# Scores of two attention heads on separate halves of TensorE's rows, with the rounded and the low parts of q in tiles of their own

## The chip, the cores and the metric

The kernel runs on one core of one Trainium2 chip. The metric is the device time of one execution in microseconds (us); the time of a kernel is the median of its runs. One further execution was recorded by the hardware profiler, and all rows below come from it. The engines are named as in the profile: PE is TensorE's matmul, PEld its load of the stationary operand (it lies beside PE), DVE is VectorE, ACT ScalarE, POOL GpSimd, SP SyncE, from which the transfers are issued.

## The reference

A decoder layer on 512 positions of 2,048 channels. One projection of the modulated input gives q, k, v, two gates and the two halves of a gated convolution. Half of the layer is attention, 16 query heads of 64 channels over 4 key heads, each block of 128 queries looking at its own and the previous block of keys:

```python
scores = jnp.einsum('bnqhgd,bnkhd->bnhgqk', qb, kw) * (HEAD_DIM ** -0.5)
...
scores = jnp.where(valid[None, :, None, None], scores + bias, jnp.finfo(f32).min)
probs = jax.nn.softmax(jnp.concatenate([scores, sink], axis=-1), axis=-1)[..., :-1]
out = jnp.einsum('bnhgqk,bnkhd->bnqhgd', probs, vw)
```

The other half is a causal convolution of width 31 with a layer norm and a pointwise product. Both halves go through one output product, a residual and a last layer norm.

## The kernel before

**Halves.** Everything is float32. [...]

**Stages.** First the input is modulated and the convolution's inputs are projected, then k and v. Then for each of four groups `j` of four query heads the projections of q and of the attention gate follow (`project`, two PSUM tiles `prj`, 96 matmuls each), and after them the convolution's gate, the output product and the rest. On DVE the depthwise convolution (line 295, `cv`) is spread between the splits of the weights.

**q.** A group's q comes out of the projection as two PSUM tiles of 128 partitions, each with two heads of 64 channels one above the other. `q_out` makes one tile `qs` of 128 partitions for each head: its rounded half on one 64 partitions, its low half on the other 64. `kh` and `kl`, the halves of k, hold the same 64 channels twice, on the lower and the upper partitions.

**Scores.** With that, one matmul over all 128 rows of TensorE gives high plus low of q times the rounded k (line 411), a second one the same q times the low k (line 413), 256 keys wide each. A block (`attention`, one group and 128 queries) is 4 heads of 2 matmuls; there are 16 blocks, 128 score matmuls in all. DVE reads each head's scores out of PSUM with the bias and a running minimum (line 417), ACT takes the exponentials and scales them (422, 426), TensorE transposes (433), the transposed probabilities are split (174, 175), and `values` multiplies by v (443 over 128 columns of the stationary operand, 445 over 64).

**Order.** A block's three stages are put between the products of the next projections (`between`, STAGES = 0, 6, 9 steps of 12 matmuls), and the framework's scheduler orders each engine's queue from there. PSUM tiles of attention are named `att`; there are five of them, and a block uses two for scores, one or two for transposes and one for the values.

Of the kernel before, what the change touches and what calls it, by code (L numbers as in the profile page):

```python
# [18 lines left out]
P = 128  # L19
S = 512  # L20
# [24 lines left out]

# smalls: columns of one [128, n] array
SM_ADA = 0
# [6 lines left out]

# the first phase goes over the contraction chunks as they come; these pairs of
# output tiles (glu_a, glu_b) stay in PSUM, the others are summed part by part.
N_FIXED = 3
# [3 lines left out]

# microseconds of other work for the vector engine with each block of weights
N_WARM = 5
# [11 lines left out]
def plan():  # L75
    """The order of the first phase: the next chunk of h, unless the tensor engine would wait for weights."""
    done = {i: 0 for i in range(N_FIXED, NC8)}
    items, fixed, n_h = [("h", 0)], 0, 1
    dma, pe = 8.5, 11.0
    while n_h < NK:  # L80
        item = None
        i = min(done, key=lambda j: (done[j], j))
        n = min(n_h - done[i], PART[1])
        if pe - dma < LEAD:
            if fixed < n_h:
                item, dma, pe = ("fix", fixed), dma + 1.1, max(pe, dma + 2) + 3.9
                fixed += 1
            elif n >= min(PART[0], n_h):
                item, dma, pe = ("rot", i, done[i], n), dma + 0.37 * n, max(pe, dma + 2) + 1.3 * n
                done[i] += n  # L90
        if item is None:
            item, dma = ("h", n_h), dma + 6.6
            n_h += 1
        items.append(item)
    items += [("fix", k) for k in range(fixed, NK)]
    # what is left of each pair, most of it first
    rest = sorted(done, key=lambda j: (done[j], j))
    return items + [("rot", i, done[i], NK - done[i]) for i in rest if done[i] < NK]


def parts_of(k0, n):
    """At most four chunks to a block."""
    m = -(-n // 4)
    cuts = [k0 + n * a // m for a in range(m + 1)]
    return list(zip(cuts[:-1], cuts[1:]))


def w_in_blocks():
    """The blocks of w_in in the order of use: (first chunk, chunks, columns)."""
    blocks = []  # L110
# [12 lines left out]
def bucket_runs():  # L123
    """(bucket, first distance, one past the last distance) for distances 0..127."""
    max_exact = N_BUCKETS // 2
# [14 lines left out]
def build(tc, xT, x, c, wadaT, smalls, win, wpw, wout, relT, sinks, ln_g, ln_b, out):  # L140
# [11 lines left out]

    # ---- the activations of c, on all partitions
    ones = pp.tile([P, P], F32, name="ones")
# [17 lines left out]
    def split(raw, hi, lo, hi_engine=None):  # L172
        """hi + lo = raw, each with 12 significant bits."""
        nc.scalar.activation(hi, raw, AF.Copy)  # L174
        nc.vector.tensor_tensor(lo, raw, hi.bitcast(F32), op=ALU.subtract)  # L175
# [15 lines left out]
    def silu_c(pool, psp, tag):  # L191
        # the products of ones that come first set the tensor engine's clock
        warm = psp.tile([P, S], F32, name="warm", tag=tag)
# [5 lines left out]
        parts = [slice(i * S, (i + 1) * S) for i in range(4)]  # L199
        # the halves of c lie where the last chunks of h come later  # L200
        chl = [(hh[0:1, NK - 4 + i, :], hl[0:1, NK - 4 + i, :]) for i in range(4)]
# [12 lines left out]
    def ada(pool, cb, js, parts=1):  # L214
        """columns js of mod: for each, 128 outputs of the adaLN product, one per partition."""
        wa = [pool.tile([P, D], F32, name="wa", bufs=WA_BUFS) for j in js]
# [9 lines left out]

    # ---- phase 1: h and the GLU projections, chunk by chunk
    glu = {}
# [55 lines left out]
    def conv_steps():  # L284
        """the depthwise convolution, two chains at a time"""
        for i0 in range(0, NC8, 2):
# [14 lines left out]
    def take(gen, budget):  # L301
        """some of the work that fills the vector engine between the splits of the weights"""
        while budget > 0:
# [13 lines left out]

    # ---- phase 2: q, k, v, the gate, and attention
    def chain(*gens):
# [10 lines left out]

    # the negated bias of each head over the distance + 128; elsewhere the mask
    rel = p2.tile([16, N_BUCKETS], F32, name="rel", bufs=1)
# [58 lines left out]
    def attention(j, qs, sg, nb, n):  # L391
        """a block of queries of four heads, in three stages"""
        blk = slice(n * P, (n + 1) * P)
# [6 lines left out]
        def scores():  # L400
            # the negated scores, and after them the negated sink
            e = kept["e"] = p2.tile([P, GRP, 2 * P + 1], F32, name="e")
            least = p2.tile([P, GRP], F32, name="least")
            total = p2.tile([P, GRP], F32, name="total")
            nc.gpsimd.tensor_copy(e[:, :, nkeys], nsink[:, heads])
            for hp in range(2):
                sp = ps2.tile([P, S], F32, name="att", bufs=5)
                for r in range(2):
                    hd = 2 * hp + r
                    o = sp[:, r * 256:(r + 1) * 256]  # L410
                    nc.tensor.matmul(o, qs[hd][:, blk], kh[:, j, k0:k0 + 256], start=r == 0, stop=False,
                                     skip_group_check=True)
                    nc.tensor.matmul(o, qs[hd][:, blk], kl[:, j, k0:k0 + 256], start=False, stop=r == 1,
                                     skip_group_check=True)
                for r in range(2):
                    hd = 2 * hp + r
                    nc.vector.tensor_tensor_reduce(e[:, hd, :nkeys], sp[:, r * 256:r * 256 + nkeys],
                                                   nb[:, hd, nkeys - 1::-1] if nkeys < 256 else nb[:, hd, ::-1], 1.0,
# [20 lines left out]
        def values():  # L439
            pv = ps2.tile([P, S], F32, name="att", bufs=5)  # L440
            for half, (pth, ptl) in enumerate(kept["p"]):
# [3 lines left out]
                nc.tensor.matmul(pv[:HD, :], v[:, 0, :], ptl, start=False, stop=half == nh - 1, skip_group_check=True)  # L445
            # the products with the low halves of the values lie in the upper partitions
            low = p2.tile([HD, S], F32, name="low", bufs=1)
# [9 lines left out]

    # the stages of attention go between the products of the next projections
    stages = {}
# [7 lines left out]
    for j in range(NKV):  # L467
        qs = [p2.tile([P, S], F32R, name="qs", bufs=8) for _ in range(GRP)]
        def q_out(t, ps):
            for r in range(2):  # L470
                dst, rows = qs[2 * t + r], slice(r * HD, (r + 1) * HD)
                other = slice((1 - r) * HD, (2 - r) * HD)
                nc.scalar.activation(dst[rows, :], ps[rows, :], AF.Copy, scale=-(HD ** -0.5))
                nc.vector.scalar_tensor_tensor(dst[other, :], ps[rows, :], -(HD ** -0.5), dst[rows, :].bitcast(F32),
                                               op0=ALU.mult, op1=ALU.subtract)

# [5 lines left out]
        nb = p2.tile([P, GRP, 256], F32, name="nb")  # L482
        # [query, head, 255 - key]
        nc.sync.dma_start(nb, bass.AP(tensor=ext_d.tensor, offset=ext_d.offset + GRP * j * 384 + 1,
# [7 lines left out]

    # ---- phase 3: the gate of the convolution, and its layer norm
    def gc_out(j):
# [26 lines left out]
    def norm_steps():  # L521
# [27 lines left out]
        ps = colsum(tot)  # L549
        # 1 / sqrt(var + eps), and one Newton step: r (1.5 - 0.5 v r^2)  # L550
        nc.scalar.activation(tot, ps, AF.Sqrt, bias=eps, scale=1.0 / D_CONV)
# [12 lines left out]
        yield None  # L564
        # the normalised channels, through silu, take the place of the last chunks of h
        for i in range(NC8):
# [33 lines left out]
    def y_split(k0):  # L600
        # y of attention takes the place of the first chunks of h
        if k0 < 8:
# [7 lines left out]

    # ---- phase 4: the output product over the channels of attention
    def w_out_block(n, kp):
# [22 lines left out]

    # ---- phase 5: the pointwise product, its bias and gate; the attention half so far into the residual
    p5 = es.enter_context(tc.tile_pool(name="p5", bufs=1, reuse_waits="tile"))
# [56 lines left out]

    # ---- phase 6: the output product over the channels of the convolution, and the last layer norm
    def yh(k):
# [12 lines left out]

    # the weights of the last two column groups take the place of h  # L710
    def late_block(n, kp):
# [19 lines left out]
    for t in range(NB):  # L731
        ts_ = slice(t * P, (t + 1) * P)
        for n in (2, 3):
            # the last product in two parts, for what follows it to start early
            parts = [slice(0, HALF), slice(HALF, S)] if (t, n) == (NB - 1, 3) else [slice(0, S)]
# [21 lines left out]
def laid_out(x, c, w_ada, b_ada, w_in, rel_bias, sinks, conv_w, conv_b, conv_ln_g, conv_ln_b, w_pw, b_pw, w_out,  # L757
             ln_g, ln_b):
    x, w_in = np.asarray(x)[0], np.asarray(w_in)[0]
    cols = lambda v, n: np.asarray(v)[0].reshape(n, P).T  # noqa: E731  # L760
    cw = np.asarray(conv_w)[0].T.reshape(NC8, P, TAPS).transpose(1, 0, 2).reshape(P, NC8 * TAPS)
# [31 lines left out]
```

## Time and profile before

| | before |
|---|---|
| median of 3 runs (lowest to highest) | 789.35 us (788.3 to 790.66) |
| span of the profiled execution | 788.9 us |
| PE busy | 760.9 us, 96% |
| PEld busy | 628.9 us, 80% |
| DVE busy | 676.0 us, 86% |
| ACT busy | 341.8 us, 43% |
| stretch with the score matmuls | about 259 to 510 us |

The span is 0.45 us under the median and inside the runs' spread, so the rows can be set against the median with that difference. Matmuls are pipelined: the duration of one row (0.39 us for 512 columns) is longer than the distance to the next one's start (0.23 us). What a matmul costs is read from distances between starts.

### The profile page before, as it was taken

The page shows a single profiled execution, that of the slowest core. Times are in us where ns is not written, and L with a number is a line of the kernel's source. Part 1 is how long each engine was busy: PE and PEld are TensorE (multiplying, and loading weights), DVE is VectorE, ACT ScalarE, POOL GpSimd, SP SyncE. Part 2 cuts the span into 40 slices and gives each one's busy share as a digit, 9 for nine tenths or more (in the row PEclk, how much of TensorE's full clock was granted, in tenths as well). Part 3 has the DMA queues.
Part 4 walks back from the last instruction along what each step waited for, and adds up shares of the span by engine and source line. Part 5 has one row for each costly group of instructions (what it writes and reads, how often), then busy time and mean ns, then how long its engine had stood idle before and what let it go on. Part 6 is the DMA issues. An engine that isn't in the chain of part 4 may idle for free.

```text
span 788.9 us, 9718 instructions
## 1 busy us (share of the span) xinstructions
PE 760.9 (96%) x3522; PEld 628.9 (80%) x3522; DVE 676.0 (86%) x1101; ACT 341.8 (43%) x574; POOL 20.5 (3%) x30
## 2 busy tenths in 40 slices
PE   5999999999999999999999999999999799999994
PEld 4787888878898888888888888888878588888883
DVE  6888988959999999999999998579795539877797
ACT  4543333333242346656756756445473145433000
POOL 0000000000230000000000100000000000000000
PEclk9999999999999999999999999999999989999997
DMA  8999988513332232322321322367667633684033
GB/s 308 414 412 410 359 324 308 185 60 109 114 134 101 86 104 95 107 67 78 107 81 54 106 81 81 102 225 222 239 215 243 221 134 123 224 302 152 0 107 107
DMA packets 39089, 136.10 MB, mean 173 GB/s; under 512 B 4337, under 2 KB 6785, under 8 KB 34817
## 3 DMA queue, kind: packets, MB, share of 16 engines
q1 hardware_dynamic: 39042, 135.49, 49.2%
q8 instruction: 27, 0.44, 0.2%
q14 instruction: 20, 0.16, 0.1%
HBM read 131.26 MB, written 4.22 MB: 172 GB/s over the span
## 4 chain that ended last, share of the span: by engine, by line
PE 80%; DVE 9%; DMA 7%; issue 2%; ACT 0%; SPq 0%; DVEq 0%
PE prj L187 14%; PE prj L188 14%; PE prj L189 14%; DMA wa<-in_wadaT 6%; PE rot L187 5%; PE rot L189 5%; PE rot L188 5%; PE att L188 4%; PE att L189 4%; PE att L187 4%; PE fix L187 3%; DVE junk L588 3%; PE fix L188 3%; PE fix L189 3%; PE att L433 2%
## 5 line engine op out<-in xcount | busy, mean ns | idle before, releaser
L174 ACT ACTIVATE wh<-wr 128x1024 fp32r<-128x1024 f32 (+2 forms) x129 | 127.3, 997 | 203.5 <-PE prj L188 109.7
L187 PE MATMUL prj<-hh,wh 128*128 128x512 f32 x480 | 188.5, 393 | 0.0
L189 PE MATMUL prj<-hh,wl 128*128 128x512 f32 x480 | 187.6, 392 | 0.0
L188 PE MATMUL prj<-hl,wh 128*128 128x512 f32 x480 | 187.5, 391 | 0.0
L175 DVE TENSOR_TENSOR wl<-wr,wh 128x1024 fp32r<-128x1024 f32 (+2 forms) x129 | 147.3, 1145 | 27.5 <-ACT wh L174 27.1
L295 DVE SCALAR_TENSOR_TENSOR cv<-u,sm,cv 128x512 f32<-128x512 f32 x240 | 169.5, 743 | 0.8
L189 PEld LDWEIGHTS prj<-hh,wl 128*128 128x128 f32 x480 | 90.2, 188 | 19.4 <-issue 0.2
L187 PEld LDWEIGHTS prj<-hh,wh 128*128 128x128 f32 x480 | 90.2, 188 | 18.8 <-issue 0.2
L188 PEld LDWEIGHTS prj<-hl,wh 128*128 128x128 f32 x480 | 90.3, 188 | 18.1
L224 DVE CUSTOM_DVE_ANT_0 junk<-wa,cb,sm 128x2048 bf16<-128x2048 f32 (+1 forms) x32 | 72.9, 2279 | 2.6 <-DMA wa<-in_wadaT 2.6
L187 PE MATMUL rot<-hh,wh 128*128 128x512 f32 x160 | 62.2, 393 | 1.7 <-DVE acc L272 1.7
L188 PE MATMUL rot<-hl,wh 128*128 128x512 f32 x160 | 62.6, 391 | 0.0
L189 PE MATMUL rot<-hh,wl 128*128 128x512 f32 x160 | 62.5, 392 | 0.0
L188 PE MATMUL att<-wl,hh 128*128 128x512 f32 (+1 forms) x144 | 50.9, 354 | 6.7 <-DVE wl L175 6.7
L189 PE MATMUL att<-wh,hl 128*128 128x512 f32 (+1 forms) x144 | 50.2, 349 | 0.0
L187 PE MATMUL att<-wh,hh 128*128 128x512 f32 (+1 forms) x144 | 48.5, 349 | 0.0
L188 PE MATMUL fix<-hl,wh 128*128 128x512 f32 x96 | 38.2, 398 | 0.0
L187 PEld LDWEIGHTS rot<-hh,wh 128*128 128x128 f32 x160 | 30.3, 189 | 9.5 <-DVE acc L272 1.7
L189 PE MATMUL fix<-hh,wl 128*128 128x512 f32 x96 | 37.8, 394 | 0.0
L188 PEld LDWEIGHTS att<-wl,hh 128*128 128x128 f32 x144 | 28.0, 194 | 11.9 <-DVE wl L175 8.6
L189 PEld LDWEIGHTS rot<-hh,wl 128*128 128x128 f32 x160 | 30.1, 188 | 6.8 <-DVE wl L175 0.3
L188 PEld LDWEIGHTS rot<-hl,wh 128*128 128x128 f32 x160 | 30.1, 188 | 6.4
(163 smaller groups left out, 1179.3 us busy)
## 6 DMA issues: line engine op xcount, KB each, us to landing
wr<-in_win SPq DMA_DIRECT2D x68, 512.0 KB, 3.4
wa<-in_wadaT SPq DMA_DIRECT2D x30, 1024.0 KB, 8.6
wa<-in_wadaT SPq DMA_DIRECT2D x36, 512.0 KB, 5.0
wr<-in_wout SPq DMA_DIRECT2D x32, 512.0 KB, 4.6
wr<-in_win SPq DMA_DIRECT2D x24, 384.0 KB, 9.0
xt<-in_xT SPq DMA_DIRECT2D x16, 256.0 KB, 9.1
wr<-in_wpw SPq DMA_DIRECT2D x8, 512.0 KB, 3.3
xs<-in_x SPq DMA_DIRECT2D x16, 256.0 KB, 5.2
```

The costliest lines, as they stand in the source:

```text
L174: nc.scalar.activation(hi, raw, AF.Copy)
L175: nc.vector.tensor_tensor(lo, raw, hi.bitcast(F32), op=ALU.subtract)
L187: nc.tensor.matmul(ps, lh, rh, start=start, stop=False)
L188: nc.tensor.matmul(ps, lh, rl, start=False, stop=False)
L189: nc.tensor.matmul(ps, ll, rh, start=False, stop=stop)
L224: nc.vector.tensor_tensor_reduce(junk[:, part], w[:, part], cb[:, part], 1.0, first, ALU.mult, ALU.add, mod[:, j:j + 1])
L295: nc.vector.scalar_tensor_tensor(cv[i][:, :S], glu[i][:, j:j + S], w, cv[i][:, :S], op0=ALU.mult, op1=ALU.add)
L433: nc.tensor.transpose(pt[:, hd * P:(hd + 1) * P], kept["e"][:, hd, half * P:(half + 1) * P], ident)
L588: nc.vector.tensor_tensor_reduce(junk, wa, cb[:, hs], 1.0, dst if half else first, ALU.mult, ALU.add, dst)
```

## The change

`q_out` now writes one tile for each of the two PSUM tiles of q with both heads' rounded halves (`qs[2 * t]`, 128 partitions, one ACT instruction) and one with both heads' low halves (`qs[2 * t + 1]`, one DVE instruction). A score matmul takes 64 partitions of such a tile: head `r` of a pair lies on rows `64 r` to `64 r + 63`. A head's scores are now three matmuls over half of the rows: rounded q by rounded k, rounded q by low k, low q by rounded k; the fourth product, low q by low k, is no longer computed. The two heads of a pair alternate, and each writes a PSUM tile of its own (`sp[r]`), with the two pairs side by side in the columns.

```diff
-            for hp in range(2):
-                sp = ps2.tile([P, S], F32, name="att", bufs=5)
-                for r in range(2):
-                    hd = 2 * hp + r
-                    o = sp[:, r * 256:(r + 1) * 256]
-                    nc.tensor.matmul(o, qs[hd][:, blk], kh[:, j, k0:k0 + 256], start=r == 0, stop=False,
-                                     skip_group_check=True)
-                    nc.tensor.matmul(o, qs[hd][:, blk], kl[:, j, k0:k0 + 256], start=False, stop=r == 1,
-                                     skip_group_check=True)
+            sp = [ps2.tile([P, S], F32, name="att", bufs=5) for _ in range(2)]
+            for hp in range(2):
+                for a, b in ((qs[2 * hp], kh), (qs[2 * hp], kl), (qs[2 * hp + 1], kh)):
+                    for r in range(2):
+                        rows = slice(r * HD, (r + 1) * HD)
+                        nc.tensor.matmul(sp[r][:, hp * 256:(hp + 1) * 256], a[rows, blk], b[rows, j, k0:k0 + 256],
+                                         start=hp == 0 and b is kh and a is qs[0],
+                                         stop=hp == 1 and a is qs[3], skip_group_check=True)
+            for hp in range(2):
                 for r in range(2):
                     hd = 2 * hp + r
-                    nc.vector.tensor_tensor_reduce(e[:, hd, :nkeys], sp[:, r * 256:r * 256 + nkeys],
+                    nc.vector.tensor_tensor_reduce(e[:, hd, :nkeys], sp[r][:, hp * 256:hp * 256 + nkeys],
...
-            for r in range(2):
-                dst, rows = qs[2 * t + r], slice(r * HD, (r + 1) * HD)
-                other = slice((1 - r) * HD, (2 - r) * HD)
-                nc.scalar.activation(dst[rows, :], ps[rows, :], AF.Copy, scale=-(HD ** -0.5))
-                nc.vector.scalar_tensor_tensor(dst[other, :], ps[rows, :], -(HD ** -0.5), dst[rows, :].bitcast(F32),
-                                               op0=ALU.mult, op1=ALU.subtract)
+            nc.scalar.activation(qs[2 * t], ps, AF.Copy, scale=-(HD ** -0.5))
+            nc.vector.scalar_tensor_tensor(qs[2 * t + 1], ps, -(HD ** -0.5), qs[2 * t].bitcast(F32), op0=ALU.mult,
+                                           op1=ALU.subtract)
```

On PE, this is what stands at the second block of scores before the change; `att` with its number is a PSUM tile, `qs` with its number a tile of q.

```order
L189 MATMUL prj_2350<-hh_71,wl_2416 128x512
L411 MATMUL att_2458<-kh_1638,qs_2041 128x256
L413 MATMUL att_2458<-kl_1639,qs_2041 128x256
L411 MATMUL att_2458<-kh_1638,qs_2042 128x256
L413 MATMUL att_2458<-kl_1639,qs_2042 128x256
L411 MATMUL att_2465<-kh_1638,qs_2043 128x256
L413 MATMUL att_2465<-kl_1639,qs_2043 128x256
L411 MATMUL att_2465<-kh_1638,qs_2044 128x256
L413 MATMUL att_2465<-kl_1639,qs_2044 128x256
L187 MATMUL prj_2349<-hh_71,wh_2450 128x512
```

And this is the same block on PE with the change, without its neighbours among the projections; of two rows that follow each other the first takes the lower 64 partitions of `qs`, the second the upper 64.

```order
L412 MATMUL att_2458<-kh_1638,qs_2041 128x256
L412 MATMUL att_2459<-kh_1638,qs_2041 128x256
L412 MATMUL att_2458<-kl_1639,qs_2041 128x256
L412 MATMUL att_2459<-kl_1639,qs_2041 128x256
L412 MATMUL att_2458<-kh_1638,qs_2042 128x256
L412 MATMUL att_2459<-kh_1638,qs_2042 128x256
L412 MATMUL att_2458<-kh_1638,qs_2043 128x256
L412 MATMUL att_2459<-kh_1638,qs_2043 128x256
L412 MATMUL att_2458<-kl_1639,qs_2043 128x256
L412 MATMUL att_2459<-kl_1639,qs_2043 128x256
L412 MATMUL att_2458<-kh_1638,qs_2044 128x256
L412 MATMUL att_2459<-kh_1638,qs_2044 128x256
```

Eight rows have become twelve, and the two PSUM tiles take turns. In the changed program all 16 blocks stand like this, as one burst of 12 between projections; before, all but the first block stood as one burst of 8.

On DVE, this is where the first group's q is taken out of PSUM before the change (`qs`), between steps of the convolution (`cv`) and splits of weights (`wl`).

```order
L474 SCALAR_TENSOR_TENSOR qs<-prj,qs 64x512
L295 SCALAR_TENSOR_TENSOR cv<-u,sm,cv 128x512 x2
L474 SCALAR_TENSOR_TENSOR qs<-prj,qs 64x512
L295 SCALAR_TENSOR_TENSOR cv<-u,sm,cv 128x512 x2
L175 TENSOR_TENSOR wl<-wr,wh 128x1024
L474 SCALAR_TENSOR_TENSOR qs<-prj,qs 64x512
L295 SCALAR_TENSOR_TENSOR cv<-u,sm,cv 128x512 x2
L474 SCALAR_TENSOR_TENSOR qs<-prj,qs 64x512
```

With the change the same place on DVE reads:

```order
L473 SCALAR_TENSOR_TENSOR qs<-prj,qs 128x512
L295 SCALAR_TENSOR_TENSOR cv<-u,sm,cv 128x512 x3
L175 TENSOR_TENSOR wl<-wr,wh 128x1024
L295 SCALAR_TENSOR_TENSOR cv<-u,sm,cv 128x512
L473 SCALAR_TENSOR_TENSOR qs<-prj,qs 128x512
```

Four instructions on 64 partitions have become two on 128, and the convolution's steps have closed up around them.

## Rows read from the trace of the kernel before

**Rows 1.** The page: busy time of each engine with its share of the span and its instructions, and the first line of the chain that ended last (share of the span by engine).

```profile
PE 760.9 (96%) x3522; PEld 628.9 (80%) x3522; DVE 676.0 (86%) x1101; ACT 341.8 (43%) x574; POOL 20.5 (3%) x30
...
PE 80%; DVE 9%; DMA 7%; issue 2%; ACT 0%; SPq 0%; DVEq 0%
```

**Rows 2.** [...]

```profile
259.00:510.00 251.00, 251.00 (x1219) 208.98 (x1218) 234.49 (x446) 150.84 (x313) 7.69 (x14) 1.00 0.26 85
```

**Rows 3.** The view of waits for PE over the whole span: who waited for whom, us in total, times, longest.

```profile
PE att L188 <- DVE wl L175: 6.7, 4, 4.2
PE fix L187 <- ACT hh L245: 6.5, 1, 6.5
PE rot L187 <- DVE acc L272: 1.7, 2, 1.3
PE warm L195 <- DVE eps L161: 1.1, 1, 1.1
PE warm L211 <- ACT cb L208: 0.7, 1, 0.7
```

**Rows 4.** The timeline of PE around one block of scores: start, duration, engine, line, operation. The left-out lines go on in the same step.

```profile
309.08 0.39 PE L189 MATMUL prj<-hh,wl 128*128 128x512 f32 x1
309.31 0.28 PE L411 MATMUL att<-kh,qs 128*128 128x256 f32 x1
309.42 0.28 PE L413 MATMUL att<-kl,qs 128*128 128x256 f32 x1
...
310.14 0.28 PE L413 MATMUL att<-kl,qs 128*128 128x256 f32 x1
310.26 0.40 PE L187 MATMUL prj<-hh,wh 128*128 128x512 f32 x1
310.49 0.40 PE L188 MATMUL prj<-hl,wh 128*128 128x512 f32 x1
```

**Rows 5.** The view by lines with shapes kept apart: count, then busy us and mean ns of one, then idle time before. First the score matmuls, then loads of a stationary operand: of scores, of the values with 128 and with 64 columns, and two of the start of the program, with one row and with 128.

```profile
L413 PE MATMUL att<-kl,qs 128*128 128x256 f32 x64 | 16.1, 283 | 0.0
L411 PE MATMUL att<-kh,qs 128*128 128x256 f32 x64 | 16.0, 282 | 0.0
...
L411 PEld LDWEIGHTS att<-kh,qs 128*128 128x128 f32 x64 | 12.1, 190 | 0.7
...
L443 PEld LDWEIGHTS att<-pth,vhl 128*128 128x128 f32 x28 | 5.3, 188 | 1.7
L445 PEld LDWEIGHTS att<-ptl,vhl 128*64 128x64 f32 x28 | 3.8, 136 | 1.2
L195 PEld LDWEIGHTS warm<-ones 128*128 128x128 f32 x10 | 2.2, 329 | 1.0 <-DVE eps L161 1.0
L207 PEld LDWEIGHTS psc<-hl,ones_r 1*128 1x128 f32 x4 | 1.3, 316 | 0.2
```

**Rows 6.** The timeline of PE where the values and the transposes of two blocks meet; the line with x8 is a run of eight transposes, merged, 1.04 us from the first one's start to the last one's end. Beside it the mean of one transpose from the view by lines.

```profile
312.78 0.39 PE L189 MATMUL prj<-hh,wl 128*128 128x512 f32 x1
313.01 0.40 PE L443 MATMUL att<-pth,vhl 128*128 128x512 f32 x1
313.24 0.40 PE L445 MATMUL att<-ptl,vhl 128*64 128x512 f32 x1
313.48 1.04 PE L433 MATMUL att<-ident,e 128*128 128x128 f32 x8
...
L433 PE MATMUL att<-ident,e 128*128 128x128 f32 x112 | 15.1, 272 | 0.0
```

**Rows 7.** The timeline of PEld at an early place where PE had come to wait for a low half (0.20 us idle), so that two loads follow each other with nothing ahead of them.

```profile
24.28 0.19 PEld L188 LDWEIGHTS fix<-hl,wh 128*128 128x128 f32 x1 [0.20 <-DVE hl L247]
24.39 0.19 PEld L189 LDWEIGHTS fix<-hh,wl 128*128 128x128 f32 x1
```

**Rows 8.** The view by lines, shapes kept apart: the instructions of `q_out`, and two on 128 partitions of the same width.

```profile
L474 DVE SCALAR_TENSOR_TENSOR qs<-prj,qs 64x512 fp32r<-64x512 f32 x16 | 11.0, 688 | 0.5
L247 DVE TENSOR_TENSOR hl<-h,hh 128x512 fp32r<-128x512 f32 x16 | 11.0, 688 | 4.2 <-ACT h L246 4.2
...
L473 ACT ACTIVATE qs<-prj 64x512 fp32r<-64x512 f32 x16 | 9.5, 593 | 11.2 <-PE prj L189 5.6 <-DVE qs L474 5.3
...
L480 ACT ACTIVATE sg<-prj 128x512 f32<-128x512 f32 x8 | 4.7, 588 | 1.7 <-PE prj L189 1.7
```

**Rows 9.** Timelines of DVE and ACT between two blocks' scores: the split of transposed probabilities, the first read of scores, and the last scaling of probabilities before the transposes of 303.4 us.

```profile
306.94 0.68 DVE L175 TENSOR_TENSOR ptl<-att,pth 128x512 fp32r<-128x512 f32 x1
310.09 0.48 DVE L417 CUSTOM_DVE_ANT_0 e<-att,nb,nsink 128x256 f32<-128x256 f32 x1 [0.31 <-PE att L413]
...
290.22 1.28 ACT L426 ACTIVATE e<-e,total 128x128 f32<-128x128 f32 x4 [0.37 <-DVE total L424]
303.40 0.60 PE L433 MATMUL att<-ident,e 128*128 128x128 f32 x4
```

## The prediction

> **What bounds the kernel now.** I read the page first: PE is busy for 96% of the span and carries 80% of the chain that ended last [rows 1]. Then the view by stretches, for the 251 us in which all scores lie: PE is busy for every one of them, at the full clock [rows 2]. Then PE's waits: five in all, 16.7 us, and every one belongs to the start, the first phase or the output product; none is for scores, transposes or values [rows 3], and the score matmuls have no idle time before them [rows 5]. So between 259 and 510 us time is the sum of the distances between PE's starts and of nothing else. DVE, 234.49 of 251 us busy there, is close behind but is not waited for. What the change is worth is therefore what it does to those distances in 16 places.
>
> **What a block of scores takes now.** From the first score's start to the next projection's start the timeline has 310.26 - 309.31 = 0.95 us for 8 matmuls, 0.119 us each [rows 4]. Sixteen blocks: 15.2 us.
>
> **What a block takes after.** Twelve matmuls of the same 256 columns, each with its own load of 128 columns, alternating between the lower and the upper rows. No row of before has a matmul on half of the rows, so the price is bounded from both sides.
>
> The low bound is that the two of a pair run together and the pair goes at the pace of one matmul now: 6 x 0.119 = 0.71 us, 0.24 us less for each block, 16 x 0.24 = 3.8 us less in all. The high bound is that they don't overlap at all: 12 x 0.119 = 1.43 us, 0.48 more, 7.6 us more in all.
>
> Between them stands the load of the stationary operand. Its pace shows in two places. Where nothing was ahead of it, one load followed another after 0.11 us [rows 7]. And eight transposes, whose moving operand has only 128 columns, take 1.04 us with 0.272 for the last, so (1.04 - 0.272) / 7 = 0.110 us from one to the next [rows 6]. Both say that a load of 128 columns holds the load path for 0.11 us. That it is columns which count shows in 188 ns for 128 against 136 for 64; that rows don't shows at the start of the program, 316 ns for a load of one row against 329 for 128 [rows 5]. So a load of half of the rows should be no shorter. Today that hides: one load of 0.11 us lies beside one matmul of 0.119. After the change twelve loads stand where eight stood. If they go one after the other, as every pair of loads in this trace does, a block takes 12 x 0.110 = 1.32 us whatever the matmuls do: 0.37 more, 16 x 0.37 = 5.9 us more. I take this value: it is the one the nearest rows speak for, and it lies 1.7 us under the high bound.
>
> **Changing from full to half rows and back.** That happens twice a block, 32 times. The nearest row is the change between a stationary operand of 128 columns and one of 64 in the values: 0.23 us to it and 0.24 us from it, where two equal matmuls of 512 columns are 0.23 apart [rows 4, 6]. That is 0.01 us at most, 32 x 0.01 = 0.3 us. The other end is that the new shape waits until the matmul before has left the array: the rows give 283 ns for a score with the next one 119 later [rows 4, 5], so 0.164 us more, and 0.39 against 0.23 for a projection, 0.16. That is 32 x 0.164 = 5.3 us. I take the low end, 0.3 us, from the row that it is nearest to. [...]
>
> **Taking q out of PSUM.** Sixteen DVE instructions of 0.688 us on 64 partitions become 8 on 128. A 128-partition instruction of this width takes 0.688 as well, so DVE has 5.5 us less to do; ACT has 8 x 0.59 = 4.7 us less [rows 8]. PE waits for neither in this stretch [rows 2, 3], so I put both at nothing. What hides the work is PE itself. If DVE were the bound, these 5.5 us would be a gain.
>
> **New waits.** A block's two PSUM tiles are now both needed with its first pair, 0.48 us earlier than the second one was. The tiles of a block go round: five in use, five there. A block's scores come 12 us apart; the split that frees a transposed tile ended at 306.94 + 0.68 = 307.62, and the next scores began at 309.31 [rows 4, 9], while the same data's first use by the values was at 313.24, 5.6 us later [rows 6]. Probabilities lay ready at 291.5 for transposes at 303.4 [rows 6, 9]. The first DVE read of scores would come up to 0.4 us later in a block, which vanishes in 12 us. So no wait arises. The work behind attention on PE stands in the same order as before, and moves as a whole.
>
> **Sum.** 5.9 + 0.3 = 6.2 us on a span of 788.9: 795.1. The runs' median lies 0.45 us above the span, so 795.5.
>
> **Rivals.**
> Side by side, changes cheap: -3.8 + 0.3 = -3.5 us, 785.9. For it: the two of a pair use different rows and different PSUM tiles, and nothing in the program makes one wait for the other. Against it: it needs two loads within 0.119 us where the trace never shows two closer than 0.11. It decides as soon as loads to different rows overlap so far that a pair takes under 0.155 us (6 x 0.155 + 0.02 is today's 0.95). [...]
> Side by side, but drained at each change: -3.8 + 5.3 = +1.5 us, 790.9. [...]
> Loads in a row, or no overlap at all, and drained: 5.9 + 5.3 = 11.2 to 7.6 + 5.3 = 12.9 us more, 800.5 to 802.2. [...] Against it: the cheap change of rows 6.
>
> **Chances.** Loads in a row with cheap changes, up to no overlap at all (794 to 798): 0.35. Side by side and cheap: 0.25. Side by side and drained: 0.20. Both costs: 0.20. The forecast is the likeliest, 795.5 us, its own range 793.5 to 798. The range for all reaches from just under the first rival to the cheaper end of the last, 785.2 to 801. A measurement of this kernel tells about 0.3% (2.4 us) from no change: faster 0.25, within 0.3% 0.20, slower 0.55.
>
> **What would show it.** Right: starts of score matmuls 0.11 us apart all through a burst of 12, loads 0.11 apart, a burst of about 1.3 us, and the projections at both its ends at their usual 0.23. Side by side would show as two starts close together, then a pause, and a burst of 0.7 us. A drain would show as 0.16 us extra between the last projection and the first score, and again after the last. DVE's busy time in the stretch should fall by 5.5 us with no effect. I am wrong if PE waits for a score's PSUM tile or for q, or if the later stalls of the output product (6.7 us for weights, rows 3) come out differently because everything ahead of them has moved.

## The result, and the profile after

The changed kernel takes 795.73 us (median of 4 runs, 794.8 to 795.97) against 790.0 (4 runs, 788.3 to 790.82) before: ratio 1.007, 95% interval 1.0048 to 1.0093. The forecast of 795.5 us is met. Its reason is not: the loads do not go one after the other. What happened comes nearest to the rival "side by side, but drained at each change": a pair of scores every 0.117 us, and 0.195 us for each change of shape where that rival had 0.164; that the engine drains there is not shown. And 795.73 is at the upper end of what this kernel does; two further sets of runs (below) have medians of 793.97 and 794.34.

Busy time of each engine and the chain by engine, from the page of the changed kernel, answering [rows 1]:

```profile
PE 764.5 (96%) x3586; PEld 624.5 (79%) x3586; DVE 669.3 (84%) x1093; ACT 336.4 (42%) x566; POOL 16.0 (2%) x30
...
PE 80%; DMA 9%; DVE 8%; issue 2%; SPq 1%; ACT 0%; DVEq 0%
```

PE has 64 instructions more (16 blocks, 12 matmuls for 8) and is busy 3.6 us longer; DVE, ACT and PEld have less to do. The bound has not moved. Next, PE's timeline around one block of scores, answering [rows 4]: start, duration, engine, line, operation; x2 and x4 are runs of two and four with like operands, merged.

```profile
311.03 0.39 PE L188 MATMUL prj<-hl,wh 128*128 128x512 f32 x1
311.26 0.39 PE L189 MATMUL prj<-hh,wl 128*128 128x512 f32 x1
311.57 0.38 PE L412 MATMUL att<-kh,qs 64*128 64x256 f32 x2
311.80 0.28 PE L412 MATMUL att<-kl,qs 64*128 64x256 f32 x2
311.92 0.40 PE L412 MATMUL att<-kh,qs 64*128 64x256 f32 x4
312.15 0.28 PE L412 MATMUL att<-kl,qs 64*128 64x256 f32 x2
312.27 0.28 PE L412 MATMUL att<-kh,qs 64*128 64x256 f32 x2
312.48 0.50 PE L187 MATMUL prj<-hh,wh 128*128 128x512 f32 x1
312.82 0.40 PE L188 MATMUL prj<-hl,wh 128*128 128x512 f32 x1
```

Two matmuls begin together (x2), and behind the second pair the pairs follow each other at 0.12 us (311.80, 311.92). Twelve take 311.57 to 312.48, 0.91 us, where eight took 0.95. But at both ends there are gaps that the kernel before lacks: 0.31 from the last projection to the first score (0.23 before), 0.23 from the first pair to the second (0.12 between the others), 0.21 from the last pair to the projection (0.12 before), and 0.34 from that projection to the next (0.23 before).

The loads of the same burst, from PEld's timeline:

```profile
311.03 0.19 PEld L189 LDWEIGHTS prj<-hh,wl 128*128 128x128 f32 x1
311.57 0.19 PEld L412 LDWEIGHTS att<-kh,qs 64*128 64x128 f32 x2 [0.35 <-PE prj L188]
311.68 0.19 PEld L412 LDWEIGHTS att<-kl,qs 64*128 64x128 f32 x2
...
312.47 0.19 PEld L187 LDWEIGHTS prj<-hh,wh 128*128 128x128 f32 x1
312.58 0.19 PEld L188 LDWEIGHTS prj<-hl,wh 128*128 128x128 f32 x1
```

Two loads take together the 0.19 us that one takes: they run side by side, which no row of before had shown. And the first load after a change starts with its matmul (311.57 and 311.57, 312.47 and 312.48), where otherwise it runs ahead (311.68 for the matmul of 311.80). PEld sits idle for 0.35 us before it.

PE's waits, answering [rows 3]; the two at the start of the program (1.8 us) are as before:

```profile
PE fix L187 <- ACT hh L245: 7.0, 1, 7.0
PE att L188 <- DVE wl L175: 6.5, 3, 3.4
PE rot L187 <- DVE acc L272: 1.7, 2, 1.3
PE prj L188 <- DVE wl L175: 1.3, 1, 1.3
```

None is for scores or q. The fourth does not stand in [rows 3]; it lies in the output product, as the second does.

In these names `hh` and `wh` are rounded halves, which ACT writes (for the weights line 174), `hl` and `wl` low halves, the rest of the same numbers, which DVE writes (line 175); lines 187 to 189 are the three matmuls of one product, rounded by rounded and the two mixed ones.

**Where the time went.** The distance that holds all 16 blocks goes from the start of the first phase's last matmul (`rot`) to the start of the output product's first (`prj<-wh,hh`); I call it the stretch. Its two ends, from PE's timeline of before:

```profile
196.51 0.39 PE L189 MATMUL rot<-hh,wl 128*128 128x512 f32 x1
...
545.78 0.39 PE L187 MATMUL prj<-wh,hh 128*128 128x512 f32 x1
```

and of the changed kernel:

```profile
198.34 0.39 PE L189 MATMUL rot<-hh,wl 128*128 128x512 f32 x1
...
550.66 0.39 PE L187 MATMUL prj<-wh,hh 128*128 128x512 f32 x1
```

349.27 us have become 352.32: 3.05 us more. In it, taken to the whole microsecond, PE is busy throughout, before and after (first before, then after; columns, as in [rows 2]: length of the stretch, busy time and instructions of PE, PEld, DVE, ACT and POOL, TensorE's granted clock as a share of full speed, DMA share, GB/s):

```profile
196.00:545.00 349.00, 349.00 (x1739) 293.74 (x1739) 327.64 (x611) 188.50 (x364) 19.36 (x16) 1.00 0.32 105
```

```profile
198.00:550.00 352.00, 352.00 (x1804) 289.21 (x1803) 321.30 (x602) 183.18 (x356) 14.83 (x16) 1.00 0.31 104
```

So the 3.05 us are distances between PE's starts at the full clock (1.00 in both lines), and no wait. The pause before a burst is no wait in disguise either: it is 0.318 or 0.319 us in all 16 blocks, whatever semaphore the first score waits for, and also in the first block, where no wait stands directly before it. The profiled spans differ by 794.0 - 788.9 = 5.1: 3.05 here, 1.83 in that `rot` ended later, 0.2 behind. Whether the 1.83 belongs to the change the further runs tell.

The 3.05 by medians over the blocks, in us:

| distance between starts | before | after | difference |
|---|---|---|---|
| last projection to first score | 0.226 | 0.318 | +0.092 |
| first score to last | 0.832 | 0.697 | -0.135 |
| last score to next projection | 0.120 | 0.204 | +0.084 |
| that projection to the one behind it | 0.234 | 0.341 | +0.107 |
| sum | 1.412 | 1.560 | +0.148 |

Within the burst the first pair stands 0.222 ahead of the second, the others 0.117 apart: 0.105 of the 0.697 is the change of shape too, and without it the burst is 0.24 shorter. So a block gains 0.24 by the pairs and loses 0.092 + 0.105 + 0.084 + 0.107 = 0.39 by two changes, 0.195 each. Over 16 blocks: -3.8 + 6.2 = +2.4 us. The ten distances behind these add 0.039 a block (2.288 before, 2.327 after), 0.63 us; the remaining 0.05 is in no single place.

What the 0.107 and the 0.039 behind a burst are, a place of the kernel before shows where no rows change. At 51 us, at the full clock (1.00 from 50 to 54 us), PE's next load has had to wait for a low half, and so it starts with its matmul instead of ahead of it. PE's timeline there, and that load from PEld's:

```profile
51.16 0.39 PE L188 MATMUL rot<-hl,wh 128*128 128x512 f32 x1
51.43 0.50 PE L189 MATMUL rot<-hh,wl 128*128 128x512 f32 x1
51.77 0.40 PE L187 MATMUL rot<-hh,wh 128*128 128x512 f32 x1
52.01 0.40 PE L188 MATMUL rot<-hl,wh 128*128 128x512 f32 x1
...
51.42 0.19 PEld L189 LDWEIGHTS rot<-hh,wl 128*128 128x128 f32 x1 [0.30 <-DVE wl L175]
```

This matmul, too, lasts 0.50 us, the next one starts 0.34 after it, and the ten distances behind that add up to 2.326. It is the picture behind a burst, without a change of rows. At 28.73 us, in a second such place, the next matmul comes after 0.334 and the ten distances are 2.288: the 0.107 came with both loads, the 0.039 with one. So I read the 0.107 as the price of a load that could not run ahead; what the traces show of the change of rows itself is that the load is held back (PEld idle for 0.35 us before 311.57), and the pauses of 0.092 and 0.084 before it. The 0.105 behind the first pair looks like the same thing, but no row separates the two there.

### The profile page after: what moved, and what is told of

Same layout as the page of the kernel before. It is cut to its first block, busy times and chain, and to the rows that moved or that the text cites. A ratio compares the mean times of both kernels' runs of the same rounds, so it can differ in the third digit from the quotient of the medians.

```text
span 794.0 us, 9829 instructions
## 1 busy us (share of the span) xinstructions
PE 764.5 (96%) x3586; PEld 624.5 (79%) x3586; DVE 669.3 (84%) x1093; ACT 336.4 (42%) x566; POOL 16.0 (2%) x30
## 4 chain that ended last, share of the span: by engine, by line
PE 80%; DMA 9%; DVE 8%; issue 2%; SPq 1%; ACT 0%; DVEq 0%
PE prj L187 14%; PE prj L188 14%; PE prj L189 14%; DMA wa<-in_wadaT 8%; PE rot L187 5%; PE rot L189 5%; PE rot L188 5%; PE att L188 4%; PE att L189 4%; PE att L187 3%; PE fix L187 3%; PE fix L188 3%; PE fix L189 3%; DVE junk L587 3%; PE att L412 2%
## 5 line engine op out<-in xcount | busy, mean ns | idle before, releaser
L187 PE MATMUL prj<-hh,wh 128*128 128x512 f32 x480 | 190.5, 397 | 0.0
L423 ACT ACTIVATE e<-e,least 128x257 f32<-128x257 f32 (+1 forms) x64 | 30.2, 474 | 23.7 <-DVE least L418 23.6
```

The costliest lines, as they stand in the source:

```text
L187: nc.tensor.matmul(ps, lh, rh, start=start, stop=False)
L423: nc.scalar.activation(e[:, hd, :nkeys + 1], e[:, hd, :nkeys + 1], AF.Exp, bias=least[:, hd:hd + 1], scale=-1.0, accum_out=total[:, hd:hd ...
```

## Experiments

Theory, formed from these rows: pairs run side by side, and each change between full and half rows costs 0.19 us. Rivals: what is lost belongs to the single matmul or load (then it does not matter how many bursts there are), or to work outside PE (q's evacuation, or what lies behind attention). The number that decides is the length of the stretch, since it repeats far better than the time of a run. The expectations count a part of it, from the end of the v projection to the end of attention: 250.70 before, 253.75 after. It differs from the stretch by a constant.

| kernel | stretch, us | against before | time, ratio to before (95%) |
|---|---|---|---|
| before, and two repeats | 349.27, 349.27, 349.27 | | 1.0007 (0.9994 to 1.002), 0.9998 (0.9987 to 1.0009) |
| after, and two repeats | 352.32, 352.32, 352.32 | +3.05 | 1.007 (1.0048 to 1.0093), 1.0053 (1.0033 to 1.0074), 1.0049 (1.0031 to 1.0068) |
| after, bursts split | 358.72 | +9.45 | 1.0148 (1.0124 to 1.0172) |
| after, two blocks in a burst | 348.14 | -1.13 | 0.9993 (0.998 to 1.0006) |
| before, stages moved as in the row above | 349.11 | -0.16 | 0.9987 (0.9973 to 1.0001) |
| after, heads not alternating | 352.43 | +3.16 | 1.0056 (1.0034 to 1.0079) |
| after, one half of the rows only | 363.41 | +14.14 | 1.0183 (1.0163 to 1.0202) |
| before, with the new `q_out` | 349.36 | +0.09 | 1.0 (0.9982 to 1.0018) |

### Both kernels again

No edit but a comment in the kernel before; the changed one as it is.

> The kernel before, unchanged but for a comment, timed against itself. The first 1,192 matmuls of both kernels stand in the same order, yet in the profile of the changed one the end of the first phase came 1.82 us later (last matmul of the first phase's fixed tiles 171.4 us instead of 169.5). If that is chance of one execution, the start of this copy may lie anywhere between, and the ratio is 1.000 within 0.002. If it belongs to the program, this copy shows 169.5 again and the changed kernel 171.4.

> The changed kernel, unchanged, in five rounds. Shape theory: pairs run side by side (16 x 0.25 = 4.0 us less) and each burst pays about 0.39 us for going to half rows and back (16 x 0.39 = 6.3 us more); with what else the stretch shows 3.1 us in all, ratio near 1.004, if the 1.82 us at the start are chance. If they belong to the program, ratio 1.006 to 1.007 as in the first timing and the end of the first phase at 171.4 us again.

> The changed kernel once more, on the same chip as the three others. In the traces so far the stretch with attention is 3.05 us longer than before in both executions, the medians differ by 4.8 and 5.7. If the stretch is all, 1.004; if something outside it belongs to the change, 1.006 or more, with the place in the trace.

> The kernel before once more, for its trace. The means of spans differ by 4.3 us between before (787.8, 50 runs) and the changed kernel (792.1, 20 runs), of which the attention stretch has 3.05. If the rest lies in the output product, the stretch from the end of attention to the pointwise product is 143 to 143.5 us in an execution near the mean of before, against 144.6 to 145.1 in the three traces of the changed kernel; if it is spread, 144 or more.

The stretch repeats to 0.01 us, while times of one kernel spread over 4 to 6 us (790.92 to 797.1 in one set of ten). The first phase's last matmul starts at 198.34, 196.16 and 197.68 us in the three traces of the changed kernel, and at 196.51, 196.75 and 196.91 in those of before; one execution of the changed kernel is earlier than all of before, so the 1.83 us of the first profile are no fixed part of the change. Over the executions whose span was recorded the mean span is 787.9 us before (90) and 792.1 after (20): 4.2 more, of which the stretch explains 3.05. In the output product PE waits for low halves of weights (`att` and `prj`, line 188) for 6.7, 6.5 and 5.5 us in the three profiles of before, and for 7.8, 7.7 and 7.4 in those of after. That would be a further 1.4 us on average. But the time from the output product's first matmul to the pointwise product's first, of which the last expectation speaks, is 144.25, 144.92 and 142.21 us in the three profiles of before and 144.49, 144.88 and 144.46 in those of after. The third of before is even shorter there than expected, the other two are as long as the changed kernel's: where the rest lies is not settled. DVE, which writes those halves, itself waits between 540 and 620 us for transfers of the modulation's weights (17.7 us in the first profile of before, 16.5 in the first of after), so it is not simply that this wait grew; and the kernel with its scores on one half, which comes to this place 11 us later still, waits for 5.2 only.

### Twice as many bursts

```diff
-STAGES = (0, 6, 9)
+STAGES = (0, 0.5, 6, 9)
...
-        def scores():
+        def half_scores(hp):
...
+        def scores_a():
...
+            half_scores(0)
...
+        def scores_b():
+            half_scores(1)
...
```

The first pair of heads is multiplied where the block's burst stood, the second six projection matmuls later, with the reductions behind it.

> The changed kernel with each block's scores in two bursts of 6, one pair of heads each, with 6 projection matmuls between: 32 bursts instead of 16, same matmuls. Shape theory: 16 more goings and comings at 0.39 us, 6.3 us slower than the changed kernel, about 1.008. My forecast's load theory (0.11 us for each load, changes 0.01 us): 0.3 us slower, ratio to the changed kernel 1.000.

The same 192 score matmuls in 32 bursts of 6: the stretch grows by 6.40 us over the changed kernel's, 0.40 for each of the 16 bursts more. PE's timeline at half a block:

```profile
297.65 0.39 PE L189 MATMUL prj<-hh,wl 128*128 128x512 f32 x1
297.97 0.39 PE L407 MATMUL att<-kh,qs 64*128 64x256 f32 x2
298.20 0.28 PE L407 MATMUL att<-kl,qs 64*128 64x256 f32 x2
298.31 0.28 PE L407 MATMUL att<-kh,qs 64*128 64x256 f32 x2
298.52 0.50 PE L187 MATMUL prj<-hh,wh 128*128 128x512 f32 x1
298.86 0.40 PE L188 MATMUL prj<-hl,wh 128*128 128x512 f32 x1
```

The four long distances (0.32, 0.23, 0.21, 0.34) are those of the longer burst. Here the price hangs on the burst, not on the matmul.

### Half as many bursts

Two blocks' scores together, on the changed kernel; the same staging on the kernel before as a control. In the control the scores of two blocks are not one burst: only in the first pair of blocks do 14 of the 16 matmuls stand together, in the others one to seven projection matmuls stand between the parts. So it shows what moving the stages is worth, and not a burst of 16.

```diff
-        for n in range(NB):
-            for f, at in zip(attention(j, qs, sg, nb, n), STAGES):
-                stages.setdefault(hook[0] + 4 * n + at, []).append(f)
+        for m in range(0, NB, 2):
+            first, second = attention(j, qs, sg, nb, m), attention(j, qs, sg, nb, m + 1)
+            for f, at in sorted(((first[0], 0), (second[0], 0), (first[1], 4), (first[2], 6),
+                                 (second[1], 6), (second[2], 9)), key=lambda p: p[1]):
+                stages.setdefault(hook[0] + 4 * m + at, []).append(f)
```

> The changed kernel with the scores of two blocks in one burst of 24, transposes and values moved to steps 4, 6 and 6, 9 of the pair: 8 bursts instead of 16, same matmuls. Shape theory: 8 x 0.39 = 3.1 us faster than the changed kernel, so level with the kernel before or up to 0.8 us faster, if the moved stages wait for nothing new. Load theory: no difference to the changed kernel.

> The kernel before with the stages moved as in the run of two blocks to a burst, score matmuls over all rows. Shape theory: a matmul over all rows pays nothing at a burst's ends, so the stretch stays at 250.7 us and the ratio at 1.000; the run of two blocks to a burst was 1.1 us shorter in this stretch than before by its half rows. If moving the stages is itself worth something, this kernel gains what that one gained.

Eight changes in and out fewer took 4.18 us off the changed kernel's stretch, where 3.1 were expected. From PE's timeline:

```profile
285.83 0.39 PE L189 MATMUL prj<-hh,wl 128*128 128x512 f32 x1
286.15 0.38 PE L412 MATMUL att<-kh,qs 64*128 64x256 f32 x2
286.37 0.28 PE L412 MATMUL att<-kl,qs 64*128 64x256 f32 x2
...
287.56 0.28 PE L412 MATMUL att<-kh,qs 64*128 64x256 f32 x2
287.77 0.50 PE L187 MATMUL prj<-hh,wh 128*128 128x512 f32 x1
```

A burst of 24 pays the two changes once (medians 0.318, 0.206, 0.337) and lasts 1.411 from first score to last; 16 full-row matmuls would take 0.832 + 8 x 0.119 = 1.784. So a burst gains 0.37 and pays 0.092 + 0.086 + 0.103 = 0.28: 0.09 for each of 8, 0.74 us. With the control's 0.16 for the staging that is 0.90 of the 1.13 us by which it beats the kernel before. Of the 1.1 us that were not expected, 0.63 are the ten distances behind a block, which here take 2.288 us as in the kernel before; the rest is open. The gain over the kernel before is real in the stretch and below what the timing tells: its interval holds 1.

### Are the pairs needed, and do halves run apart?

In the first kernel the loops are swapped, so that a head's three matmuls follow each other on its half of the rows before the other head's; in the second every score matmul takes the lower half (its attention is therefore not the reference's).

```diff
-                for a, b in ((qs[2 * hp], kh), (qs[2 * hp], kl), (qs[2 * hp + 1], kh)):
-                    for r in range(2):
+                for r in range(2):
+                    for a, b in ((qs[2 * hp], kh), (qs[2 * hp], kl), (qs[2 * hp + 1], kh)):
```

```diff
-                        rows = slice(r * HD, (r + 1) * HD)
+                        rows = slice(0, HD)
```

> The changed kernel with the three matmuls of the lower head first and then the three of the upper one, in each half of a burst: the same 192 matmuls in the same 16 bursts, but neighbours now mostly use the same rows. Shape theory (halves on different rows run together, issue is in order): of 12 matmuls only the three pairs at the seams still overlap, 9 steps of 0.117 us instead of 6, 16 x 0.35 = 5.6 us slower than the changed kernel; 11.2 us if nothing overlaps at the seams. Load theory (each load 0.11 us whatever its rows): no difference to the changed kernel.

> The changed kernel with both heads of a pair taken from the lower 64 partitions, so that all 12 matmuls of a burst use the same half of the rows; the upper head's scores are then those of the lower one and the attention is not the reference's; the number and size of all operations is the changed kernel's. Shape theory, as the run without pairs has left it (each half of the rows takes its matmuls one after the other at 0.117 us, the two halves side by side whatever the order): 12 steps of 0.117 us in place of 6, 16 x 0.70 = 11.2 us longer than the changed kernel in the attention stretch (253.75 us), ends of the bursts unchanged. Load theory (0.11 us for each load, whatever the rows): no difference to the changed kernel.

The second came out as expected: 11.09 us over the changed kernel's stretch. PE's timeline of one block:

```profile
297.68 0.39 PE L189 MATMUL prj<-hh,wl 128*128 128x512 f32 x1
298.00 0.50 PE L412 MATMUL att<-kh,qs 64*128 64x256 f32 x2
298.34 0.39 PE L412 MATMUL att<-kl,qs 64*128 64x256 f32 x2
298.57 0.64 PE L412 MATMUL att<-kh,qs 64*128 64x256 f32 x4
...
299.28 0.40 PE L412 MATMUL att<-kh,qs 64*128 64x256 f32 x2
299.61 0.50 PE L187 MATMUL prj<-hh,wh 128*128 128x512 f32 x1
```

From 298.34 two matmuls take 0.23, nearly 0.12 each: on one half they go one by one, and twelve last 1.407 from first start to last, almost the 1.43 of my high bound. The distances at the two ends are the changed kernel's. So in these runs the change of shape and the running side by side are separate things, and the second comes with a half for each head: 0.697 us from first score to last with two halves, 1.407 with one.

The first kernel's expectation failed. The stretch should have grown by several us; it grew by 0.11. The timeline of the same place says why:

```profile
297.65 0.39 PE L189 MATMUL prj<-hh,wl 128*128 128x512 f32 x1
297.97 0.39 PE L412 MATMUL att<-kh,qs 64*128 64x256 f32 x2
298.19 0.29 PE L412 MATMUL att<-kl,qs 64*128 64x256 f32 x2
298.31 0.40 PE L412 MATMUL att<-kh,qs 64*128 64x256 f32 x4
...
298.88 0.50 PE L187 MATMUL prj<-hh,wh 128*128 128x512 f32 x1
```

In the program the order is `kh`, `kl`, `kh` for the lower rows and then the same for the upper. By start times it is `kh`, `kh`, `kl`, `kl`: the upper half's first matmul starts 0.01 us after the lower half's first, ahead of two that stand before it in the program. I had taken it that matmuls start in program order. (Whether the engine changes the order or a step ahead of it, the trace does not show.) In this run each half took its own matmuls in turn, and not alternating them, at this distance of three, cost 0.11 us in the whole stretch.

### The evacuation of q alone

The kernel before with the new `q_out` and its old score loop, which then multiplies the wrong halves (its attention is not the reference's).

```diff
-            for r in range(2):
-                dst, rows = qs[2 * t + r], slice(r * HD, (r + 1) * HD)
...
+            nc.scalar.activation(qs[2 * t], ps, AF.Copy, scale=-(HD ** -0.5))
+            nc.vector.scalar_tensor_tensor(qs[2 * t + 1], ps, -(HD ** -0.5), qs[2 * t].bitcast(F32), op0=ALU.mult,
+                                           op1=ALU.subtract)
```

> The change of q_out alone: 8 instructions on 128 partitions in place of 16 on 64 on ACT and on DVE, with the kernel before's score matmuls over all rows, so that its scores mix the heads' halves and its attention is not the reference's; every other operation is there. If DVE's 5.5 us are hidden as I said: ratio 1.000, and the stretch from the end of the projection of v to the end of attention as long as before (250.7 us). If DVE sets the pace there: up to 5.5 us faster, 0.993.

DVE has 319.83 us to do in 348 of the stretch, by the view by stretches, and ACT 184.05 (327.64 in 349 and 188.50 before):

```profile
197.00:545.00 348.00, 348.00 (x1735) 292.58 (x1734) 319.83 (x601) 184.05 (x356) 18.62 (x16) 1.00 0.32 105
```

The stretch stays (+0.09) and so does the time. So all but 0.09 of the 3.05 us come from the scores.

## Why the prediction was right in its number and wrong in its reason

**What bounds the kernel: right.** In the stretch time is the sum of distances between PE's starts, before and after; the 16 places account for +2.4 of 3.05 us, and the ten distances behind each for another 0.63.

**The twelve matmuls: wrong, and the step that failed.** It is the sentence that loads go one after the other "as every pair of loads in this trace does", at 0.110 each, +5.9 us. No row of that trace shows two loads in succession on separate halves of the rows, so it could not speak on the matter, and I took silence for evidence. Measured: two loads together in the time of one, a pair every 0.117 us, -3.8 us, the low bound (6 x 0.119 for a burst). PEld's x2 at 311.57, 0.19 us for both, shows it, and I had it before me as a rival.

**The change between full and half rows: wrong, and too low even at its upper end.** I took 0.01 us from the values, where 128 columns become 64, and had 0.164 as the other end. Measured: 0.195, 32 of them, 6.2 us instead of 0.3. The other end, that the new shape waits until the matmul before has left the array, was my estimate, and it fits the long distances here only in part: the first score starts 0.32 us after a projection whose row lasts 0.39, and since the ends of such rows are modelled, they do not show an engine run empty. That narrowing columns cost 0.01 (0.24 us where 0.23 is usual) was a row of the same trace and remains so; it was the wrong row to be nearest to. The 0.164 was too small although the wait that it stood for is smaller, 0.09 before the first of the new shape: it left out another 0.105 behind it, about the 0.11 us by which one load follows another [rows 7], while that load is seen to start with its matmul rather than ahead of it. For the way back to full rows the place at 51.43 us of the kernel before bears out that this second part is the load that could not go ahead; the rows were there for the forecast and I did not read them. For the first pair no row separates the two.

The two errors have opposite signs: -9.7 and +5.9 us. What is left of my 6.2 is 2.4.

**q out of PSUM, put at nothing: right**, shown by the run with `q_out` alone. **No new wait for scores: right.**

**What lies around.** I put 0.45 us between the profiled span and the median. Every timed execution lies about 2 us above its own span; the profiled 788.9 was merely one of the longer spans (mean 787.9). From 789.9 as the base, the measured 3.05 give 792.95, within 1.4 us of the two later medians. The 1.15 us that the mean spans have beyond the stretch may lie where I said I could be wrong, in the output product's stalls; but three profiles of each kernel overlap there, and the cause stays open. So the number came out through errors that nearly cancel and some unexplained time, not through the mechanism. The kernel is slower, by 0.4% as the stretch has it and 0.5% to 0.7% as the three sets of runs do.

## What to carry to other kernels

In these runs the half-row matmuls of two heads doubled up (a pair every 0.117 us) whether or not the program alternated them, but a burst of them paid 0.39 us for getting in and out among full-row work, and a head gained only 0.06 (0.24 for four), so by these numbers it would take some seven heads in one burst to break even, an estimate. Before packing small matmuls, count the changes of shape, not the matmuls, and put the bursts together first. And when no row of the trace has the new shape, a nearest row that was never in a position to show the effect is no evidence against it: its bound belongs in the range, not at the likeliest place.

## What the runs showed of the hardware that I had not expected

- Loads of 128 columns to the two halves of the rows ran at the same time in the changed kernel: 0.19 us for both (x2 at 311.57 and 311.68), what one load on 128 rows takes.
- Matmuls to the two halves left program order in the run with heads not alternating: three for the upper rows started beside three for the lower that stand ahead of them in the program, 0.01 us apart (x2 at 297.97).
- A change between 128 and 64 rows cost 0.195 us in the changed kernel, at the full clock (0.39 for the two of a burst of 12, medians of 16 blocks). A further burst of 6 cost 0.40 for its two. A burst of 24 has the same distances at its ends (0.318 before it, 0.206 and 0.337 behind it), and so has a burst of 12 on one half (0.32 before it, 0.33 from the projection behind it to the next). A change between 128 and 64 columns cost 0.01 (0.24 us where 0.23 is usual, [rows 6]).
- A load that could not run ahead of its matmul cost about 0.11 us at the full clock also among full-row matmuls (the matmul at 51.43 us of the kernel before has 0.34 us to the next instead of 0.23). That is about half of the 0.195 of a change of rows.
